# Weights and x of a hybrid decoder layer stored in HBM in the order in which SBUF holds them

## Chip, cores and metric

One core of one Trainium2 chip runs the kernel. The metric is the device time of one execution in microseconds (us). Three executions of the kernel before took 1139.64, 1139.92 and 1135.62 us, so the median is 1139.64 us. A fourth execution, the profiled one, took 1134.39 us; the trace is of that one, and its span from the first to the last instruction is 1132.3 us.

## What is computed

One decoder layer over 256 tokens of width 1024, in float32. A mixer with three groups of heads (gated linear attention, differential attention, retention) comes first, then a mixture of 32 experts of which each token takes four. Cut to what matters here:

```python
z = x @ w_in                                   # 1024 x 3344
a = concat(gla(z), diff_attention(z), retention(z)) @ w_out
x = layer_norm(alpha * x + a)
top_v, top_i = top_k(x @ w_router + b_router, 4)
for e in range(32):                            # for the tokens that chose e
    gu = x @ w_gate_up[e] + b_gate_up[e]       # 1024 x 2048
    g, u = min(gu[:, ::2], 7), clip(gu[:, 1::2], -7, 7)
    y += gate * (((u + 1) * g * sigmoid(1.702 * g)) @ w_down[e] + b_down[e])   # 1024 x 1024
ple = sigmoid(x @ w_ple_gate + b_ple_gate) * (p @ w_ple_proj)
out = layer_norm(alpha * x + y + ple)
```

`lay_out` rearranges inputs on the host, ahead of the launch; that is not in the measured time.

## The kernel before

**Units.** Every weight passes through a ring of 22 SBUF slots, each `[128, 2048]` float32, which is 1 MB: 8 KB in each of 128 partitions. A load of one slot is called a unit here. An expert has eight units of `w_gate_up`, `("gu", e, k)`, and four of `w_down`, `("dn", e, i)`. The mixer has 13 units of `w_in`, `("z", c)`, and four of `w_out`; `x` is one unit; the per-layer embedding (PLE) has four units of `w_ple_gate`, `("ple", i)`, and beside them four loads of 256 KB of `w_ple_proj`.

**Order.** `want` (L163) puts units into a list in the order in which they are to be loaded, `pump` (L170) gives the next of the list a slot whenever one is free, and `done` (L180) frees a slot after its last reader. All loads are issued by SyncE (SP) on one queue. The list is: `w_in` in the order of `zorder` (L262), `w_out`, `x`, then for expert after expert the eight units of `w_gate_up` of e and the four of `w_down` of e-1; with experts 9 to 12 the PLE units are mixed in. The transfers of one queue land in the order of their issue, some lines that the profile shows apart.

**Layout before.** `w_gate_up` is taken as it lies in HBM: row k*128+p of an expert has 2048 numbers, so partition p of a unit is one piece of 8 KB (`load_flat`, L243). The other weights have narrower rows, and a unit takes several rows for each partition:

- `load_rows2` (L221) for `w_down` and `w_out`: two pieces of 4 KB for each partition.
- `load_cols` (L211) for `w_in` and `load_colblock` (L228) for `w_ple_gate` and the first three units of the last expert's `w_down`: eight pieces of 1 KB.
- `load_cols` with `parts=2` for the second unit of `w_in` (`O_RG`), and `load_halves` (L235) for the last unit of the last `w_down`: halves of 512 KB in pieces of 512 bytes.
- `load_first_cols` (L269): the first unit of `w_in` (`O_GO`) and the transposed x (`xT`), in four quarters of 256 KB each, in turn, in pieces of 1 KB.

```python
            v = u.rearrange("p (k c) -> p k c", k=2)
            nc.sync.dma_start(v, src.rearrange("(k p) c -> p k c", p=P))
```

**Compute.** The mixer splits each `w_in` unit into two float32r parts (ACT, `split` L406; DVE, L407) and multiplies (L417, L418, L420, L432 to L435); its first unit goes unsplit (`z_unsplit`, L444). Nine matmuls on zeros run ahead of that (`keep_warm`, L381). Of the experts, `expert_up` (L1100) takes the eight `w_gate_up` units one after the other, eight matmul records for each, and frees each after its use; `expert_down` (L1127) does the same with the four units of `w_down`, eight records for each. The order in the loop is up(e), combining of a finished pair, down(e-1), activation of e. An expert with over 64 tokens takes an extra branch (`over_gather` L1143, `over_up` L1166). The last expert's `w_down` is taken by column blocks in `last_down` (L1406), each with its share of the final layer norm.

Of the kernel before, what the change touches and what calls it, by code (L numbers as in the profile page):

```python
# [69 lines left out]


def shape_constants():
    c = np.zeros((P, C_BIG), np.float32)
# [33 lines left out]
def lay_out(inp):  # L107
# [14 lines left out]
    for g in range(4):  # L122
# [4 lines left out]

    bgu = a["b_gate_up"][0].reshape(NE, 4, 2, P, 2).transpose(3, 4, 2, 1, 0)
    return {
        "x": a["x"], "xT": a["x"][0].T, "pT": a["p"][0, 0].T, "w_in": a["w_in"], "w_out": a["w_out"],  # L130
        "diff_lambda": a["diff_lambda"], "params": r, "bgu": bgu.reshape(P, 512),
        "w_gate_up": a["w_gate_up"], "w_down": a["w_down"], "b_down": a["b_down"],
        "w_ple_gate": a["w_ple_gate"], "w_ple_proj": a["w_ple_proj"],
        "ln2": np.concatenate([a["ln2_g"], a["ln2_b"]], axis=1), "big": big, "small": small, "lmask": lmask,
# [4 lines left out]
def kernel(ctx, tc, x, xT_in, pT_in, w_in, w_out, diff_lambda, params, bgu_in, w_gate_up,  # L139
                      w_down, b_down, w_ple_gate, w_ple_proj, ln2, big, small, lmask_in, out, debug=None):  # L140
    nc = tc.nc
# [65 lines left out]

    O_GQ, O_GV, O_GO, O_DQ, O_DK, O_DV = 0, 256, 528, 784, 1296, 1808
    O_RQ, O_RK, O_RV, O_RG = 2320, 2576, 2832, 3088
# [18 lines left out]
    def load_colblock(src):  # L228
        def fn(u):
            v = u.rearrange("p (k c) -> p k c", k=NK)  # L230
            nc.sync.dma_start(v, src.rearrange("(k p) c -> p k c", p=P))
            return v
        return fn

    def load_halves(src):  # L235
        def fn(u):
            v = u.rearrange("p (c w) -> p c w", c=8)
            for sl in (slice(0, 128), slice(128, 256)):
                nc.sync.dma_start(v[:, :, sl], src[:, sl].rearrange("(c p) w -> p c w", p=P))
            return v  # L240
        return fn
# [11 lines left out]
    def load_x(u):  # L253
        v = u.rearrange("p (t d) -> p t d", t=NT)
        nc.sync.dma_start(v, x[0].rearrange("(t p) d -> p t d", p=P))
        return v

    def load_ln2(u):
        nc.sync.dma_start(u[0:1, :], ln2)
        return u  # L260

    zorder = [O_GO, O_RG, O_GQ, O_RQ, O_RK, O_GV, O_RV, O_DQ, O_DK, O_DQ + 256, O_DK + 256, O_DV, O_DV + 256]  # L262

# [5 lines left out]
    def load_first_cols(u):  # L269

        v = u.rearrange("p (k c) -> p k c", k=NK)
        for q in range(4):
            sl, rows = slice(2 * q, 2 * q + 2), slice(256 * q, 256 * q + 256)
# [4 lines left out]
    for c in zorder:  # L278
        want(("z", c), load_first_cols if c == O_GO else load_cols(c, 2 if c == O_RG else 1))
        if c == O_RG:  # L280
            aside(lambda: load_first())
        if c == O_GQ:
            aside(lambda: load_second())
    for i in WORDER:
        want(("wo", i), load_rows2(w_out[0, i * 256:(i + 1) * 256, :]))
    want("xs", load_x)
# [4 lines left out]
    for e in range(NRUN + 1):  # L291
# [3 lines left out]
        if e >= 1:  # L295
            for i in range(4):
                sl = slice(i * 256, (i + 1) * 256)
                if e < NRUN:
                    fn = load_rows2(w_down[0, e - 1, sl, :])
                else:  # L300
                    fn = (load_halves if i == 3 else load_colblock)(w_down[0, e - 1, :, sl])
                units.append((("dn", e - 1, i), fn))
# [4 lines left out]
        if e in PLE_AT:  # L307
            i = PLE_AT.index(e)
            if i == 0:
                units += [("x1T", lambda u: u), ("plt", lambda u: load_pT(u))]  # L310
            units.append((("ple", i), load_colblock(w_ple_gate[0, :, i * 256:(i + 1) * 256])))
        for key, fn in units:
# [97 lines left out]
    def z_transposed(c):  # L410
        u = loaded["z", c].rearrange("p (k c) -> p k c", k=NK)
# [800 lines left out]
    def general():  # L1212

        n_max = load_count(cnt[0:1, NE:NE + 1])
        with tc.If(n_max > NSLOT + NOVER):
# [9 lines left out]
            with tc.For_i(0, NRUN, 1) as ie:  # L1225
# [3 lines left out]
                with tc.If(n > NSLOT + NOVER):  # L1229
                    with tc.For_i(0, (n - (NSLOT + 1)) // NOVER, 1):  # L1230
# [27 lines left out]
    def load_pT(u):  # L1258
        pT, w0, w1, sg = carve(u, (2, S), (2, 256), (2, 256), (2, S))
        nc.sync.dma_start(pT, pT_in.rearrange("(k p) t -> p k t", p=P))  # L1260
        return pT, (w0, w1), sg

    def load_proj(i):
        nc.sync.dma_start(loaded["plt"][1][i % 2],
                          w_ple_proj[0, :, i * 256:(i + 1) * 256].rearrange("(k p) c -> p k c", p=P))

# [133 lines left out]
    def last_down(c0, n):  # L1400
        w, o, h = loaded["dn", f, c0 // 256], c0 % 256, n // 2
        py = ps_z("pyl")
        for c in range(8):
            blk, j = c // 2, c % 2
            for hf in range(2):
                nc.tensor.matmul(py[hf * 64:(hf + 1) * 64, :h], act[:, j * 4 + blk, :],  # L1406
                                 w[:, c, o + hf * h:o + (hf + 1) * h], start=c == 0, stop=c == 7)
        nc.scalar.copy(y[64:128, c0:c0 + h], py[0:64, :h])
# [48 lines left out]
```

## Time and profile before

| what | value |
|---|---|
| median of three executions | 1139.64 us |
| profiled execution | 1134.39 us |
| its span | 1132.3 us |
| PE busy | 1038.6 us, 92% of the span |
| DVE, ACT busy | 396.5 us, 194.1 us |
| mean granted TensorE clock | 0.976 |
| moved by DMA | 433.61 MB, mean 383 GB/s |
| DMA packets | 100299: 33325 under 2 KB, 67409 under 8 KB |

PE is TensorE's matmul stream, and "idle before" in a row is the time in which the engine stood still ahead of it. The ends of matmuls are modelled: a group's last record is drawn some tenths of a microsecond past the point at which the next could start. DMA share is the mean busy share of the 16 DMA engines; it passes 1.00 where packets overlap. GB/s counts what they moved. A granted clock of 1.00 is 2.4 GHz, 0.50 is 1.2 GHz.

### The profile page before, as it was taken

To read this page: it belongs to the slowest core of one execution; us is meant where nothing else is said; L and a number is where in the kernel's file an instruction comes from. 1 tells how busy PE (TensorE), PEld (TensorE's weight loads), DVE (VectorE), ACT (ScalarE), POOL (GpSimd) and SP (SyncE) were. 2 spreads that over 40 slices of the span, in tenths; PEclk is the share of its full clock that TensorE was granted. 3 is DMA by queue.
4 is the path that set the end of the run, shared out by engine and by line. 5 is a ranking of instruction groups with operands and counts; after the bars stand their busy time and mean duration, and the time that the engine had idled before them with its cause. 6 is when DMAs were issued, how large, how long until landed. Compare 5 with 4: busy or idle time off the path is not lost. (4 is left out here: it accounts for less than half of the span.)

```text
span 1132.3 us, 13655 instructions
## 1 busy us (share of the span) xinstructions
PE 1038.6 (92%) x5358; PEld 515.0 (45%) x5358; DVE 396.5 (35%) x809; ACT 194.1 (17%) x377; POOL 7.5 (1%) x19
## 2 busy tenths in 40 slices
PE   9999989999999989999899999799988799999996
PEld 7988844433433354554433343234322343334344
DVE  4977642333333241232223233223232223232235
ACT  4457431101110120101101111001010110102011
POOL 1000000000000000000000000000000000000000
PEclk9999999999999999999999999899999799999998
DMA  9956877999999999999999999999999999999991
GB/s 316 359 235 258 319 312 278 415 416 414 417 416 417 416 404 406 407 411 411 417 416 417 415 417 415 415 416 416 415 416 417 415 417 401 386 416 416 415 373 58
DMA packets 100299, 433.61 MB, mean 383 GB/s; under 512 B 6957, under 2 KB 33325, under 8 KB 67409
## 3 DMA queue, kind: packets, MB, share of 16 engines
q1 hardware_dynamic: 100002, 431.36, 95.3%
q8 instruction: 88, 1.44, 0.5%
q0 software_dynamic: 176, 0.53, 0.1%
q14 instruction: 33, 0.27, 0.1%
HBM read 430.81 MB, written 1.06 MB: 381 GB/s over the span
## 5 line engine op out<-in xcount | busy, mean ns | idle before, releaser
L1100 PE MATMUL pgu<-u,xe 128*64 128x512 f32 x2048 | 475.5, 604 | 15.4 <-DMA u<-in_w_gate_up_dram 8.9
L1100 PEld LDWEIGHTS pgu<-u,xe 128*64 128x64 f32 x2048 | 161.1, 139 | 307.1 <-issue 271.4
L1127 PE MATMUL py<-u,u 128*64 128x512 f32 x992 | 234.9, 605 | 27.8 <-DVEq L1361 18.0
L1127 PEld LDWEIGHTS py<-u,u 128*64 128x64 f32 x992 | 79.6, 139 | 166.7 <-issue 125.0
L1109 DVE COPY u<-pgu 128x512 f32<-128x512 f32 x32 | 22.1, 692 | 332.1 <-PE pgu L1100 330.8
L1055 DVE TENSOR_TENSOR u<-ptg,bgu 128x512 f32<-128x512 f32 x32 | 22.1, 692 | 236.7 <-PE ptg L1115 236.7
L1108 ACT COPY u<-pgu 128x512 f32<-128x512 f32 x32 | 18.7, 585 | 449.1 <-PE pgu L1100 430.2
L1132 ACT COPY u<-py 64x512 f32<-64x512 f32 x31 | 17.9, 578 | 277.7 <-PE py L1127 277.7
L407 DVE TENSOR_TENSOR u<-u,u 128x1024 fp32r<-128x1024 f32 x32 | 39.0, 1222 | 17.5 <-ACT u L406 17.5
L1090 DVE TENSOR_TENSOR u<-u,pcb 128x512 f32<-128x512 f32 x60 | 37.7, 682 | 13.9 <-PE pcb L1089 13.8
L406 ACT CAST u<-u 128x1024 fp32r<-128x1024 f32 x32 | 33.5, 1048 | 29.6 <-PE pzt L418 9.7
L417 PE MATMUL pzt<-u,u 128*128 128x256 f32 x128 | 32.8, 291 | 0.3 <-ACT u L406 0.3
L1276 PE MATMUL pleg<-u,u 128*128 128x256 f32 x128 | 31.0, 397 | 2.1 <-ACT u L972 2.1
L418 PE MATMUL pzt<-u,u 128*128 128x256 f32 x128 | 32.3, 287 | 0.0
L1089 PE MATMUL pcb<-u,PT 128*128 128x512 f32 x120 | 32.0, 408 | 0.0
L1022 PE MATMUL pgx<-Pm,xnh 128*128 128x256 f32 (+1 forms) x128 | 30.9, 284 | 0.0
L1115 PEld LDWEIGHTS ptg<-ci,u 128*128 128x128 f32 x128 | 17.8, 207 | 27.7 <-issue 26.9
L1022 PE MATMUL pgx<-Pm,xnl 128*128 128x256 f32 (+1 forms) x128 | 30.0, 278 | 0.0
L1276 PEld LDWEIGHTS pleg<-u,u 128*128 128x128 f32 x128 | 24.9, 199 | 6.3 <-ACT u L972 2.2
L1057 ACT ACTIVATE u<-u 128x512 f32<-128x512 f32 x32 | 19.9, 623 | 44.1 <-DVE u L1056 44.1
L1022 PEld LDWEIGHTS pgx<-Pm,xnh 128*128 128x128 f32 x128 | 24.1, 188 | 6.5 <-issue 4.1
L1089 PEld LDWEIGHTS pcb<-u,PT 128*128 128x128 f32 x120 | 21.0, 188 | 11.7 <-ACT u L1108 4.9
(290 smaller groups left out, 954.9 us busy)
## 6 DMA issues: line engine op xcount, KB each, us to landing
u<-in_w_gate_up_dram SPq DMA_DIRECT2D x256, 1024.0 KB, 18.7
u<-in_w_down_dram SPq DMA_DIRECT2D x127, 1024.0 KB, 20.0
u<-in_w_in_dram SPq DMA_DIRECT2D x11, 1024.0 KB, 12.6
u<-in_w_out_dram SPq DMA_DIRECT2D x4, 1024.0 KB, 10.8
u<-in_w_ple_gate_dram SPq DMA_DIRECT2D x4, 1024.0 KB, 20.6
u<-in_xT_dram SPq DMA_DIRECT2D x4, 256.0 KB, 4.7
u<-in_w_in_dram SPq DMA_DIRECT2D x4, 256.0 KB, 4.7
u<-in_w_in_dram SPq DMA_DIRECT2D x2, 512.0 KB, 7.5
```

The costliest lines, as they stand in the source:

```text
L406: nc.scalar.copy(wh, half)
L407: nc.vector.tensor_tensor(wl, half, wh.bitcast(F32), op=ALU.subtract)
L417: nc.tensor.matmul(pz[:, j, :], wh[:, k, :], xh[:, k, :], start=k == 0, stop=False)
L418: nc.tensor.matmul(pz[:, j, :], wh[:, k, :], xl[:, k, :], start=False, stop=False)
L1022: nc.tensor.matmul(pg[:, j, :n], v[:, t, ch], hot, start=t + i == 0, stop=t + i == NT)
L1055: nc.vector.tensor_tensor(g, pg, bg, op=ALU.add)
L1089: nc.tensor.matmul(pcb, PT[:, t * P:(t + 1) * P], v[:, sl], start=i == 0, stop=i == 1)
L1090: nc.vector.tensor_tensor(yacc[:, t, sl], yacc[:, t, sl], pcb, op=ALU.add)
L1100: nc.tensor.matmul(pgu[b][hf * 64:(hf + 1) * 64, :], xe[:, k, c0:c0 + NSLOT], w[:, b * 1024 + hf * 512:b * 1024 + (hf + 1) * 512], start=k ...
L1109: nc.vector.tensor_copy(gs[:, 1, :], pgu[1])
L1127: nc.tensor.matmul(py[nb * 64:(nb + 1) * 64, :], act[:, j * 4 + blk, :], w[:, f % 2, nb * 512:(nb + 1) * 512], start=f == 0, stop=f == 7)
L1276: nc.tensor.matmul(pg[:, j, :], w[:, k, sl], x1T[:, k, :], start=k == 0, stop=k == NK - 1)
```

## The change

Every transfer of a weight or of x becomes one piece for each partition. `lay_out` stores each unit as a `[128, 2048]` block, partition after partition, so a unit is 1 MB in one run of HBM, 8 KB for each partition. The halves of the second `w_in` unit and of the last `w_down` unit become blocks of 4 KB for each partition, the quarters of `xT` and of the first `w_in` unit, and the loads of `pT` and `w_ple_proj`, 2 KB for each partition. The transposed `w_in` units are stored by column halves, so that `split` reads 1024 numbers in a row where it read eight runs of 128; what lies in the slots is otherwise the same. The last expert's `w_down` is stored a second time, by columns (`w_last`). `w_gate_up`, the constants and the small parameters stay as they are. The number of loads, their sizes and their order stay, too.

```diff
+    by_rows = lambda m, n: m.reshape(-1, n, P, m.shape[-1]).transpose(0, 2, 1, 3).reshape(-1, P, n * m.shape[-1])
+    cols = lambda m, c, n: by_rows(m[:, c:c + n], m.shape[0] // P)[0]
+    halves = lambda m, c: np.concatenate([cols(m, c, P), cols(m, c + P, P)], axis=1)
...
-        "w_gate_up": a["w_gate_up"], "w_down": a["w_down"], "b_down": a["b_down"],
-        "w_ple_gate": a["w_ple_gate"], "w_ple_proj": a["w_ple_proj"],
+        "w_gate_up": a["w_gate_up"], "w_down": np.stack([by_rows(w, 2) for w in a["w_down"][0]]),
+        "w_last": np.stack([cols(w_last, 256 * i, 256) for i in range(3)] + [halves(w_last, 768)]),
+        "b_down": a["b_down"],
+        "w_ple_gate": np.stack([cols(w_pg, 256 * i, 256) for i in range(4)]),
+        "w_ple_proj": np.stack([cols(w_pp, 256 * i, 256) for i in range(4)]),
...
-    def load_cols(c0, parts):
+    def load_cols(c, parts):
         def fn(u):
-            v = u.rearrange("p (k c) -> p k c", k=NK)
-            src = w_in[0, :, c0:c0 + 256].rearrange("(k p) c -> p k c", p=P)
-            n = 256 // parts
+            n, src = 2048 // parts, w_in[ZORDER.index(c)]
             for i in range(parts):
-                nc.sync.dma_start(v[:, :, i * n:(i + 1) * n], src[:, :, i * n:(i + 1) * n])
+                nc.sync.dma_start(u[:, i * n:(i + 1) * n], src[:, i * n:(i + 1) * n])
             return u
         return fn
...
-    def load_rows2(src):
+    def load_blocks(src, k):
         def fn(u):
-            v = u.rearrange("p (k c) -> p k c", k=2)
-            nc.sync.dma_start(v, src.rearrange("(k p) c -> p k c", p=P))
-            return v
-        return fn
...
+            nc.sync.dma_start(u, src)
+            return u.rearrange("p (k c) -> p k c", k=k)
...
-            nc.sync.dma_start(xT[:, sl, :], xT_in[rows].rearrange("(k p) t -> p k t", p=P))
-            nc.sync.dma_start(v[:, sl, :], w_in[0, rows, O_GO:O_GO + 256].rearrange("(k p) c -> p k c", p=P))
+            nc.sync.dma_start(xu[:, sl], xT_in[:, sl])
+            nc.sync.dma_start(u[:, sl], w_in[ZORDER.index(O_GO)][:, sl])
...
-                    fn = load_rows2(w_down[0, e - 1, sl, :])
+                    fn = load_blocks(w_down[e - 1, i], 2)
...
-        parts = [split(u[:, :, j * P:(j + 1) * P]) for j in range(2)]
+        parts = [split(u[:, j]) for j in range(2)]
```

The order of instructions is the same on every engine; only the shapes of SP's loads differ. SP's first loads before (`u_69` is `xT`, `u_95` the unit `O_GO`, `u_104` the unit `O_RG`):

```order
5 L274 DMA u_69<-in_xT_dram 128x2x256
6 L275 DMA u_95<-in_w_in_dram 128x2x256
7 L274 DMA u_69<-in_xT_dram 128x2x256
8 L275 DMA u_95<-in_w_in_dram 128x2x256
9 L217 DMA u_104<-in_w_in_dram 128x8x128 x2
```

and of the change:

```order
5 L277 DMA u_69<-in_xT_dram 128x512
6 L278 DMA u_95<-in_w_in_dram 128x512
7 L277 DMA u_69<-in_xT_dram 128x512
8 L278 DMA u_95<-in_w_in_dram 128x512
9 L231 DMA u_104<-in_w_in_dram 128x1024 x2
```

Each load keeps its place and its size, and its second dimension (the pieces of a partition) is gone. The same on SP where expert 9's `w_down` and the first PLE loads stand, before:

```order
163 L224 DMA u_4009<-in_w_down_dram 128x2x1024
164 L1338 UNCONDITIONAL_BRANCH
165 L224 DMA u_4015<-in_w_down_dram 128x2x1024
166 L224 DMA u_4021<-in_w_down_dram 128x2x1024
167 L224 DMA u_4027<-in_w_down_dram 128x2x1024
168 L1260 DMA u_4038<-in_pT_dram 128x2x256
169 L231 DMA u_4105<-in_w_ple_gate_dram 128x8x256
```

and of the change:

```order
163 L238 DMA u_4009<-in_w_down_dram 128x2048
164 L1339 UNCONDITIONAL_BRANCH
165 L238 DMA u_4015<-in_w_down_dram 128x2048
166 L238 DMA u_4021<-in_w_down_dram 128x2048
167 L238 DMA u_4027<-in_w_down_dram 128x2048
168 L1262 DMA u_4038<-in_pT_dram 128x512
169 L238 DMA u_4105<-in_w_ple_gate_dram 128x2048
```

Nothing moved; two pieces of 1024 numbers became one of 2048, and eight pieces of 256 one of 2048.

## Rows read from the trace of the kernel before

**Rows 1.** The page's 40 slices (28.3 us each): DMA share, GB/s

```profile
DMA  9956877999999999999999999999999999999991
GB/s 316 359 235 258 319 312 278 415 416 414 417 416 417 416 404 406 407 411 411 417 416 417 415 417 415 415 416 416 415 416 417 415 417 401 386 416 416 415 373 58
```

**Rows 2.** Stretches: us, busy of PE, PEld, DVE, ACT, POOL; PEclk, DMA share, GB/s

```profile
0.00:194.50 194.50, 185.24 (x1258) 142.43 (x1260) 116.92 (x289) 88.05 (x187) 7.48 (x19) 0.99 0.82 296
...
400.00:811.00 411.00, 376.99 (x1752) 175.45 (x1749) 119.88 (x219) 47.13 (x83) 0.00 (x0) 0.98 1.02 413
811.00:885.00 74.00, 61.87 (x268) 19.85 (x264) 15.62 (x28) 5.94 (x10) 0.00 (x0) 1.00 1.02 417
904.00:958.00 54.00, 49.63 (x306) 20.78 (x299) 16.48 (x37) 5.05 (x9) 0.00 (x0) 1.00 1.02 417
```

**Rows 3.** PE in order of time: start, us, what, count, [idle before <-releaser]

```profile
396.23 1.94 PE L1100 MATMUL pgu<-u,xe 128*64 128x512 f32 x8 [0.55 <-DMA u<-in_w_gate_up_dram]
...
717.38 1.94 PE L1100 MATMUL pgu<-u,xe 128*64 128x512 f32 x8 [0.56 <-DMA u<-in_w_gate_up_dram]
...
834.16 1.94 PE L1100 MATMUL pgu<-u,xe 128*64 128x512 f32 x8 [0.56 <-DMA u<-in_w_gate_up_dram]
836.64 1.94 PE L1100 MATMUL pgu<-u,xe 128*64 128x512 f32 x8 [0.54 <-DMA u<-in_w_gate_up_dram]
...
846.84 7.09 PE L1127 MATMUL py<-u,u 128*64 128x512 f32 x32 [1.23 <-DVEq L1361]
...
882.58 1.94 PE L1127 MATMUL py<-u,u 128*64 128x512 f32 x8 [0.61 <-DMA u<-in_w_down_dram]
```

**Rows 4.** PE's waits from 811 to 885 us: total us, times, longest

```profile
PE pgu L1100 <- DMA u<-in_w_gate_up_dram: 5.4, 9, 1.0
PE py L1127 <- DMA u<-in_w_down_dram: 4.2, 8, 0.6
```

**Rows 5.** PE's waits from 885 us to the end, the two largest

```profile
PE pox L1143 <- DVE Pr L965: 5.4, 1, 5.4
PE py L1127 <- DVEq L1361: 4.3, 3, 1.6
```

**Rows 6.** Stretches with pieces of 8, 4, 8, 4 and 1 KB alone

```profile
285.50:302.50 17.00, 15.43 (x86) 8.66 (x84) 5.42 (x10) 2.84 (x5) 0.00 (x0) 1.00 1.02 421
306.00:312.50 6.50, 5.47 (x32) 2.31 (x28) 3.07 (x6) 1.21 (x2) 0.00 (x0) 1.00 1.03 410
...
546.50:560.00 13.50, 11.76 (x54) 3.56 (x50) 0.00 (x0) 0.49 (x1) 0.00 (x0) 1.00 1.01 417
...
467.00:472.00 5.00, 3.04 (x16) 2.17 (x17) 1.98 (x3) 0.47 (x1) 0.00 (x0) 1.00 1.02 409
...
24.00:45.00 21.00, 21.00 (x173) 20.13 (x172) 18.69 (x48) 11.02 (x18) 2.34 (x2) 1.00 1.10 349
```

**Rows 7.** SP's loads: count, KB each, median us to landing

```profile
u<-in_w_gate_up_dram SPq DMA_DIRECT2D x256, 1024.0 KB, 18.7
```

**Rows 8.** PE, then ACT, in the first 16 us, in order of time

```profile
1.17 4.02 PE L381 MATMUL pwm<-u 128*128 128x512 bf16 x9 [1.17 <-DVE u L384]
4.98 7.67 PE L444 MATMUL pzu<-u,u 128*128 128x256 f32 x32
12.93 0.39 PE L417 MATMUL pzt<-u,u 128*128 128x256 f32 x1 [0.28 <-ACT u L406]
...
11.83 1.04 ACT L406 CAST u<-u 128x1024 fp32r<-128x1024 f32 x1 [1.96 <-DMA u<-in_w_in_dram]
```

**Rows 9.** Line 406: ns min/median/max, first and last start, form

```profile
L406 ACT CAST u<-u x32: 1033/1047/1075, 11.8 to 130.8; 128x1024 fp32r<-128x1024 f32 x32
```

**Rows 10.** SP in order of time, a PLE load pair

```profile
463.64 9.61 SPq L1264 DMA_DIRECT2D u<-in_w_ple_proj_dram  x1
```

**Rows 11.** The two stretches at the lower clock, as in rows 2

```profile
890.00:904.00 14.00, 12.43 (x60) 8.26 (x64) 1.08 (x4) 2.26 (x8) 0.00 (x0) 0.51 1.02 410
...
958.00:966.00 8.00, 8.00 (x19) 2.35 (x19) 2.20 (x5) 0.00 (x0) 0.00 (x0) 0.57 0.77 307
```

More of the change, by code (lines that the diff above doesn't have):

```diff
@@ L69 @@
 R_ALL = R_RBROW + 32
+O_GQ, O_GV, O_GO, O_DQ, O_DK, O_DV = 0, 256, 528, 784, 1296, 1808
+O_RQ, O_RK, O_RV, O_RG = 2320, 2576, 2832, 3088
+ZORDER = (O_GO, O_RG, O_GQ, O_RQ, O_RK, O_GV, O_RV, O_DQ, O_DK, O_DQ + 256, O_DK + 256, O_DV, O_DV + 256)
+NATURAL = (O_GV, O_RV, O_DV, O_DV + 256)
 def shape_constants():
@@ L128, in lay_out @@
     bgu = a["b_gate_up"][0].reshape(NE, 4, 2, P, 2).transpose(3, 4, 2, 1, 0)
+    by_rows = lambda m, n: m.reshape(-1, n, P, m.shape[-1]).transpose(0, 2, 1, 3).reshape(-1, P, n * m.shape[-1])
+    cols = lambda m, c, n: by_rows(m[:, c:c + n], m.shape[0] // P)[0]
+    halves = lambda m, c: np.concatenate([cols(m, c, P), cols(m, c + P, P)], axis=1)
+    w_in, w_last, w_pg, w_pp = a["w_in"][0], a["w_down"][0, NE - 1], a["w_ple_gate"][0], a["w_ple_proj"][0]
     return {
-        "x": a["x"], "xT": a["x"][0].T, "pT": a["p"][0, 0].T, "w_in": a["w_in"], "w_out": a["w_out"],
-        "diff_lambda": a["diff_lambda"], "params": r, "bgu": bgu.reshape(P, 512),
-        "w_gate_up": a["w_gate_up"], "w_down": a["w_down"], "b_down": a["b_down"],
-        "w_ple_gate": a["w_ple_gate"], "w_ple_proj": a["w_ple_proj"],
+        "x": by_rows(a["x"][0], NT)[0], "xT": by_rows(np.ascontiguousarray(a["x"][0].T), NK)[0],
+        "pT": by_rows(np.ascontiguousarray(a["p"][0, 0].T), 2)[0],
+        "w_in": np.stack([(cols if c in (O_GO, *NATURAL) else halves)(w_in, c, *([256] if c in (O_GO, *NATURAL) else []))
+                          for c in ZORDER]),
+        "w_out": by_rows(a["w_out"][0], 2),
+        "diff_lambda": a["diff_lambda"], "params": r, "bgu": bgu.reshape(P, 512),
+        "w_gate_up": a["w_gate_up"], "w_down": np.stack([by_rows(w, 2) for w in a["w_down"][0]]),
[3 more added lines that the diff above has]
+        "w_ple_proj": np.stack([cols(w_pp, 256 * i, 256) for i in range(4)]),
         "ln2": np.concatenate([a["ln2_g"], a["ln2_b"]], axis=1), "big": big, "small": small, "lmask": lmask,
@@ L139 @@
 def kernel(ctx, tc, x, xT_in, pT_in, w_in, w_out, diff_lambda, params, bgu_in, w_gate_up,
-                      w_down, b_down, w_ple_gate, w_ple_proj, ln2, big, small, lmask_in, out, debug=None):
+                      w_down, w_last, b_down, w_ple_gate, w_ple_proj, ln2, big, small, lmask_in, out, debug=None):
     nc = tc.nc
@@ L236, in fn @@
         def fn(u):
[L237 to L240, printed above, removed]
+            for sl in (slice(0, 1024), slice(1024, 2048)):
+                nc.sync.dma_start(u[:, sl], src[:, sl])
+            return u.rearrange("p (h c w) -> p c h w", h=2, c=8)
         return fn
@@ L253, in load_x @@
     def load_x(u):
-        v = u.rearrange("p (t d) -> p t d", t=NT)
-        nc.sync.dma_start(v, x[0].rearrange("(t p) d -> p t d", p=P))
-        return v
+        nc.sync.dma_start(u, x)
+        return u.rearrange("p (t d) -> p t d", t=NT)
     def load_ln2(u):
@@ L269, in load_first_cols @@
     def load_first_cols(u):
-        v = u.rearrange("p (k c) -> p k c", k=NK)
+        xu = xT.rearrange("p k t -> p (k t)")
         for q in range(4):
-            sl, rows = slice(2 * q, 2 * q + 2), slice(256 * q, 256 * q + 256)
-            nc.sync.dma_start(xT[:, sl, :], xT_in[rows].rearrange("(k p) t -> p k t", p=P))
-            nc.sync.dma_start(v[:, sl, :], w_in[0, rows, O_GO:O_GO + 256].rearrange("(k p) c -> p k c", p=P))
+            sl = slice(512 * q, 512 * q + 512)
+            nc.sync.dma_start(xu[:, sl], xT_in[:, sl])
+            nc.sync.dma_start(u[:, sl], w_in[ZORDER.index(O_GO)][:, sl])
         return u
-    for c in zorder:
+    for c in ZORDER:
         want(("z", c), load_first_cols if c == O_GO else load_cols(c, 2 if c == O_RG else 1))
@@ L284 @@
     for i in WORDER:
-        want(("wo", i), load_rows2(w_out[0, i * 256:(i + 1) * 256, :]))
+        want(("wo", i), load_blocks(w_out[i], 2))
     want("xs", load_x)
@@ L296 @@
             for i in range(4):
-                sl = slice(i * 256, (i + 1) * 256)
                 if e < NRUN:
-                    fn = load_rows2(w_down[0, e - 1, sl, :])
+                    fn = load_blocks(w_down[e - 1, i], 2)
                 else:
-                    fn = (load_halves if i == 3 else load_colblock)(w_down[0, e - 1, :, sl])
+                    fn = load_halves(w_last[i]) if i == 3 else load_blocks(w_last[i], NK)
                 units.append((("dn", e - 1, i), fn))
@@ L310 @@
                 units += [("x1T", lambda u: u), ("plt", lambda u: load_pT(u))]
-            units.append((("ple", i), load_colblock(w_ple_gate[0, :, i * 256:(i + 1) * 256])))
+            units.append((("ple", i), load_blocks(w_ple_gate[i], NK)))
         for key, fn in units:
@@ L1400, in last_down @@
     def last_down(c0, n):
-        w, o, h = loaded["dn", f, c0 // 256], c0 % 256, n // 2
+        w, h = loaded["dn", f, c0 // 256], n // 2
+        w = w[:, :, c0 % 256 // P] if n == P else w
         py = ps_z("pyl")
@@ L1406, in last_down @@
                 nc.tensor.matmul(py[hf * 64:(hf + 1) * 64, :h], act[:, j * 4 + blk, :],
-                                 w[:, c, o + hf * h:o + (hf + 1) * h], start=c == 0, stop=c == 7)
+                                 w[:, c, hf * h:(hf + 1) * h], start=c == 0, stop=c == 7)
         nc.scalar.copy(y[64:128, c0:c0 + h], py[0:64, :h])
```

19 lines of the change are left out of this document (5 added, 14 removed).

## The prediction, made blind

> **What bounds the kernel now.** I read the slices first: the rate of the transfers is uneven for seven slices, 235 to 359 GB/s, and from the eighth on (198 us) almost flat at 404 to 417 GB/s until the end, with the share of the 16 DMA engines at its top [rows 1]. The stretches say the same: up to 194.5 us the DMA engines are busy 0.82 of the time, from 400 us on 1.02 [rows 2]. So the queue is starved of free slots in the mixer and the first experts, where TensorE sets the pace (185 of 194.5 us busy), and from 194.5 us to the last load it never runs dry.
>
> A queue that is never dry need not bound anything, since the ring can hold units that TensorE does not want yet. So the next view is PE in order of time, and PE's waits. Where TensorE is ahead, its eight records of a unit start 2.48 us after the last eight (834.16 to 836.64 us), each time released by the landing; where it is not, it needs (7.09 - 1.94) / 3 = 1.72 us for a unit, from the four units in the row at 846.84 us [rows 3]. The reader should see two things. First, TensorE catches up with the transfers in three places: three waits around 396 us, four around 717 us, and seventeen between 811 and 885 us [rows 3, 4]. Secondly, the last such wait ends at 882.58 us [rows 3]; of the nine kinds of wait that PE has after 885 us none is for a DMA; the two largest are for DVE's index work ahead of an overflowing expert and at a branch [rows 5].
>
> Thus the run has three parts: to 194.5 us TensorE's pace; to 882.6 us the transfers' pace, since whatever TensorE did in between, it stood waiting for a landing at 882.6; and then some 250 us at TensorE's pace again. **What a faster transfer gives is counted from 194.5 to 882.6 us and nowhere else.**
>
> **The change, part by part.** The sum is made against the profiled execution's 1134.39 us.
>
> *`w_down`, two pieces of 4 KB to one of 8 KB.* The trace has both sizes in one queue. Stretches with 8 KB pieces alone ran at 421 and 417 GB/s, weighted 419.2; those with 4 KB alone at 410 and 409, weighted 409.6 [rows 6]. A unit of 1.0486 MB takes 2.501 us at the one and 2.560 us at the other: 0.059 us saved. The loads from `dn` 2 to `dn` 23 lie between the two marks, 22 x 4 = 88 units: 88 x 0.059 = 5.2 us. Ends: 417 against 410 gives 0.043 us and 3.8 us; 421 against 409 gives 0.073 us and 6.4 us. The new block is read just as a `w_gate_up` unit is, 8 KB for each partition in one run of 1 MB, so I take the 8 KB rate as it stands.
>
> *PLE.* Four units and five loads of 256 KB go from 1 KB to 8 KB and 2 KB. Their stretches are mixed with others, so the price of 1 KB is taken from the `w_in` loads, 349 GB/s or 3.00 us a unit [rows 6]: 4 x (3.00 - 2.50) = 2.0 us. For the 1.25 MB in small loads, between 0 (2 KB no better than 1 KB) and 0.6 us (as good as 8 KB); I take the middle, 0.3 us. The slices give a second price: the five with PLE run at 404, 406, 407, 411 and 411 GB/s where their neighbours run at 417 [rows 1], short by 46 x 28.3 / 417 = 3.1 us in all. Together 2.3 us, ends 2.0 and 3.1.
>
> *The first microseconds.* TensorE spends 1.17 to 5 us on matmuls on zeros, then 7.67 us on 16 unsplit products in 32 records, stands 0.28 us, and starts the second unit at 12.93 us, when ACT has split what landed at 11.8 us [rows 8]. The eight quarters and the first 512 KB half land sooner with larger pieces, but TensorE can't start before its zeros are done, and the 32 records need most of those 7.67 us for themselves. Bounds: 0, and 1.0 us (the 0.28 us and the little by which the records are spread). I take 0.6 us, nearer to the visible wait and some of the spread. It shifts the whole first part, so it adds to the rest.
>
> *What costs nothing.* The rest of `w_in`, `w_out` and `x`, 16 units, lands faster and lies in the first part, under TensorE's pace; if that cover were gone (TensorE faster there), some 0.5 us for each `w_in` unit would be gained, so it is no loss in any case. `w_last` lies behind 885 us, where PE waits for no DMA [rows 5]; it can only land sooner. SP's own instructions get cheaper, as a PLE load of 256 KB held SP for 9.61 us [rows 10], and still the queue didn't run dry, because a unit lands 18.7 us after its issue [rows 7] at 2.5 us for each, some seven in flight. ACT's split takes 1033 to 1075 ns over 32 instructions, strided and contiguous halves alike [rows 9], so the new storage order of the halves gives nothing. No instruction is added or moved, so no wait is new.
>
> *Sum.* 5.2 + 2.3 = 7.5 us to 882.6 us, plus 0.6: 8.1 us, ends 5.8 and 10.5. TensorE must be able to follow. It had 3 + 4 + 17 = 24 waits of about 2.48 - 1.72 = 0.76 us, some 18 us, and the transfers give back 7.5; it will still stand waiting near 882.6, with fewer waits, and what is late next there is still `w_down` and `w_gate_up`. So 1134.39 - 8.1 = 1126.3 us for an execution like the profiled one. That one was 5.25 us under the median of 1139.64; at the median, **1131.5 us**.
>
> The Trainium skill speaks against this sum: its page "DMA: Bandwidth & Descriptors", section "Rules for kernel authors", wants 128 partitions and at least 1 MiB for each DMA, and nothing more, for most of the bandwidth. All the units had that before, so by the rule the change would bring next to nothing (rival 1, its second case); the trace disagrees, since units of one size differ by 2% with the piece [rows 6].
>
> **The rivals.** A difference of 0.5% (5.7 us) is about what a measurement can tell from no change.
>
> *1. Only part of `w_down`'s lower rate belongs to the piece.* A 4 KB stretch always follows a switch from one tensor to another, which stays. If half of the 2% stays, `w_down` gives 2.6 us, and with half of PLE and the same start 2.6 + 1.2 + 0.6 = 4.4 us: 1135.2 us, no change that can be told. If all of it stays, in PLE too, 0.6 us is left: 1139.0 us, which is the case of the rule above. Against both: both rates hold flat over stretches of 5 to 17 us, and the 1 KB stretch lies in line (349) [rows 6]. The Trainium skill, "DMA: Bandwidth & Descriptors", section "Why small descriptors are slow (HBM only)", names a fixed overhead of about three bus cycles a descriptor at 32 bytes a cycle; worked out from that, as an estimate, two pieces of 4 KB cost 262 cycles against 259, 1.2%, and 88 units would give 2.6 us. By the rows the price is twice that.
>
> *2. TensorE becomes the bound before 882.6 us.* It has some 10 us in hand (18 against 7.5). Spells at the lower clock could use that up; 20 us more at 1.2 GHz would, and each 2 us beyond take 1 us of the gain. For it: 0.98 mean clock from 400 to 811 us [rows 2]. A case in its middle keeps half, 4 us: 1135.6 us.
>
> *3. Slower: the clock.* After 885 us the run goes at TensorE's pace, and there two stretches, 14.0 us at 0.51 and 8.0 us at 0.57 [rows 11], lie around the overflowing expert, where TensorE had stood for 5.4 us waiting for DVE [rows 5]. Together they cost 14.0 x 0.49 + 8.0 x 0.43 = 10.3 us. If the shifted arrivals leave other gaps there and the clock comes back later, every us more at 1.2 GHz costs half a us: 16 us more eat the gain, 28 us more make the kernel slower by 0.5%, 1145 us with 28. Against it: the work from 885 us on is the same, and from 904 to 958 us it ran at 1.00 [rows 2].
>
> *4. More.* If TensorE has less to wait for, it may also lose fewer spells, and 8 KB at 421 GB/s without the switch would make it 10 to 12 us: 1128.5 us.
>
> That the pieces don't become larger is excluded by the shapes of SP's loads.
>
> **How the numbers follow.** The forecast 0.72, rival 1 0.11 (0.02 of it for nothing at all), rival 2 0.05, rival 3 0.04, rival 4 0.08. The forecast's own range is its ends, 1139.64 - 10.5 = 1129.1 to 1139.64 - 5.8 = 1133.8 us; its lower end moves to 1124.5 us if executions come out as the profiled one did (1126.3, and a little below), its upper to 1136 us with rivals 1 and 2. So 1124.5 to 1136 us. Faster by over 0.5% (under 1133.9 us): most of the forecast (0.68), rival 4 and a little of rivals 1 and 2, 0.77; within 0.5% 0.19; slower 0.04, rival 3.
>
> **What would show it.** In the profile after: packets under 8 KB fall from 67409 to under 14000; the GB/s digits are flat near 419 from the eighth slice on, without the dip at PLE; waits of PE for DMA remain between 800 and 885 us, fewer than seventeen, the last ending near 874 us; the stretch from there to the end is as long as before, some 250 us. I am wrong if the flat rate stays at 410 in `w_down`'s stretches (rival 1), if PE has no DMA wait after 700 us (rival 2), or if the stretch behind the last wait grew (rival 3).

## The result and the profile after

| | before | change |
|---|---|---|
| median of seven executions each, side by side | 1139.63 us | 1129.34 us |
| lowest and highest | 1133.74, 1139.92 us | 1128.16, 1130.85 us |
| profiled execution, its span | 1134.39, 1132.3 us | 1130.51, 1128.5 us |

The ratio, taken over the executions side by side, is 0.9924, with a 95% interval of 0.9905 to 0.9943: about 8.7 us (6.5 to 10.8), where 8.1 us were forecast. The two medians lie 10.3 us apart; that of the kernel before stands near the top of its seven executions here, and in the later series it is 1136.0 to 1138.2 us. The change's median lies 2.2 us under the 1131.5 us forecast, well inside the range. The two traced executions differ by 3.9 us only: that of before was near the low end of its kernel's scatter, that of the change in the upper half of its own. So what follows compares stretches of traces, and times only as ratios.

The page of the change, its slices and its packets, to be read against [rows 1]:

```profile
GB/s 350 365 199 226 314 304 282 404 420 420 420 419 420 419 419 419 419 420 403 420 407 421 419 420 420 418 419 420 419 420 420 420 421 408 403 419 421 420 351 38
DMA packets 62411, 433.61 MB, mean 384 GB/s; under 512 B 6957, under 2 KB 7469, under 8 KB 10705
```

Packets under 8 KB fell from 67409 to 10705. From the ninth slice on the rate stands at 418 to 421 GB/s, but for the slices from 930 us on that were low before, too, and two lone slices, 403 and 407, which are new and are taken up further down. The dip of the five PLE slices, 404 to 411, is gone.

The stretches of [rows 2], and then two short ones with `w_gate_up` alone and `w_down` alone, as in [rows 6]; columns as there:

```profile
0.00:194.50 194.50, 184.84 (x1244) 142.89 (x1244) 117.61 (x288) 88.02 (x187) 7.41 (x19) 0.98 0.77 294
400.00:811.00 411.00, 378.90 (x1770) 177.96 (x1768) 119.89 (x219) 47.26 (x83) 0.00 (x0) 0.98 1.01 418
811.00:885.00 74.00, 61.24 (x272) 21.74 (x268) 20.15 (x36) 8.05 (x13) 0.00 (x0) 0.99 1.01 420
...
605.20:621.30 16.10, 15.70 (x72) 6.61 (x68) 7.00 (x12) 1.83 (x3) 0.00 (x0) 1.00 1.01 419
624.30:631.70 7.40, 6.37 (x34) 2.67 (x30) 1.72 (x3) 0.58 (x1) 0.00 (x0) 1.00 1.02 418
```

From 400 to 811 us the DMA share is about what it was, 1.01 against 1.02; it now carries 418 GB/s instead of 413, and `w_down` runs as `w_gate_up` does. In landings: the median spacing of a `w_down` unit was 2.548 us and is 2.487 us, that of a `w_gate_up` unit stays at 2.49 us.

PE's waits from 811 to 885 us, then from 885 us to the end, as [rows 4] and [rows 5]:

```profile
PE pgu L1102 <- DMA u<-in_w_gate_up_dram: 3.8, 6, 1.1
PE py L1129 <- DMA u<-in_w_down_dram: 2.2, 4, 0.6
...
PE pox L1145 <- DVE Pr L967: 5.4, 1, 5.4
PE py L1129 <- DVEq L1362: 4.3, 3, 1.6
```

Ten waits for transfers are left of seventeen (thirteen in a second trace of the change), and those around 396 and 717 us [rows 3] are gone. Behind 885 us the same two waits lead, to the tenth. PE in order of time, the end of the stretch that the transfers bound, as [rows 3]:

```profile
834.17 1.94 PE L1102 MATMUL pgu<-u,xe 128*64 128x512 f32 x8 [0.54 <-DMA u<-in_w_gate_up_dram]
836.65 1.94 PE L1102 MATMUL pgu<-u,xe 128*64 128x512 f32 x8 [0.55 <-DMA u<-in_w_gate_up_dram]
...
841.87 7.09 PE L1129 MATMUL py<-u,u 128*64 128x512 f32 x32 [1.23 <-DVEq L1362]
...
877.73 1.94 PE L1129 MATMUL py<-u,u 128*64 128x512 f32 x8 [0.53 <-DMA u<-in_w_down_dram]
```

The last wait for a landing ends at 877.73 us, where it ended at 882.58. TensorE still stands waiting for `w_down` there, so the transfers still bound the run up to that point.

Where did it come from? I measure from the landing of the second `w_gate_up` unit of expert 3, behind which at least two loads are always under way, to the landing of the last `w_down` unit of expert 23, the one that this last wait waits for: 684.25 us before, 675.87 us after. That is 8.4 us gained between 200 and 880 us. The span shrank by less, because 3.5 us were lost ahead of that stretch and 1.0 us behind it (882.58 to 1132.3 is 249.7 us, 877.73 to 1128.5 is 250.8). These two losses are those of this pair of traces: in a second pair, further down, that first landing is only 0.8 us later. Of the 3.5 us, 0.8 us show in the first microseconds and some 1.7 us, half of 3.4, are a spell at 1.2 GHz in the mixer, shown in the last section; the rest is open. The first microseconds, PE and then ACT, as [rows 8]:

```profile
4.98 2.75 PE L446 MATMUL pzu<-u,u 128*128 128x256 f32 x8
8.15 5.42 PE L446 MATMUL pzu<-u,u 128*128 128x256 f32 x24 [0.42 <-DMA u<-in_w_in_dram]
13.72 0.39 PE L419 MATMUL pzt<-u,u 128*128 128x256 f32 x1
...
10.44 0.62 ACT L391 CAST u<-u 128x512 fp32r<-128x512 f32 x1 [1.13 <-DMA u<-in_xT_dram]
12.62 1.05 ACT L408 CAST u<-u 128x1024 fp32r<-128x1024 f32 x1 [1.57 <-DMA u<-in_w_in_dram]
```

TensorE starts the second `w_in` unit at 13.72 us, not at 12.93, and ACT's first split, 11.83 us before, starts at 12.62 us: what the eight quarters bring lands later, with pieces twice as large. Behind the last wait, too, there is a spell at 1.2 GHz that the trace of the kernel before does not have, 3.4 us long and so worth some 1.7 us (columns as in [rows 2]):

```profile
1016.50:1021.00 4.50, 4.50 (x16) 1.29 (x14) 0.00 (x0) 0.09 (x1) 0.00 (x0) 0.62 1.01 421
```

### The profile page after: what moved, and what is told of

It reads as the page before. It is cut to its first block, busy times and chain, and to the rows that moved or that the text cites. A ratio compares the mean times of both kernels' runs of the same rounds, so it can differ in the third digit from the quotient of the medians.

```text
span 1128.5 us, 13655 instructions
## 1 busy us (share of the span) xinstructions
PE 1041.2 (92%) x5358; PEld 520.7 (46%) x5358; DVE 397.3 (35%) x809; ACT 194.1 (17%) x377; POOL 7.4 (1%) x19
## 5 line engine op out<-in xcount | busy, mean ns | idle before, releaser
L1102 PE MATMUL pgu<-u,xe 128*64 128x512 f32 x2048 | 473.3, 603 | 10.6 <-DMA u<-in_w_gate_up_dram 4.1
L1129 PE MATMUL py<-u,u 128*64 128x512 f32 x992 | 236.5, 608 | 25.8 <-DVEq L1362 16.7
L419 PE MATMUL pzt<-u,u 128*128 128x256 f32 x128 | 34.0, 299 | 0.1
L420 PE MATMUL pzt<-u,u 128*128 128x256 f32 x128 | 33.6, 296 | 0.0
## 6 DMA issues: line engine op xcount, KB each, us to landing
u<-in_w_gate_up_dram SPq DMA_DIRECT2D x256, 1024.0 KB, 16.7
u<-in_w_last_dram SPq DMA_DIRECT2D x3, 1024.0 KB, 20.5
```

The source lines that it names most:

```text
L1102: nc.tensor.matmul(pgu[b][hf * 64:(hf + 1) * 64, :], xe[:, k, c0:c0 + NSLOT], w[:, b * 1024 + hf * 512:b * 1024 + (hf + 1) * 512], start=k ...
L1129: nc.tensor.matmul(py[nb * 64:(nb + 1) * 64, :], act[:, j * 4 + blk, :], w[:, f % 2, nb * 512:(nb + 1) * 512], start=f == 0, stop=f == 7)
```

## The experiments

Two theories stood against each other. **Mine:** a unit's time depends on the size of its pieces, wherever it stands in the queue, and what is saved from 200 to 880 us is the gain. **The rival:** a `w_down` stretch is slower because the queue switches tensors there, or because of which tensor it is. The late start was a third question. The experiments came in three groups, each with its own executions of the kernel before beside it.

**`w_down` alone**, on the kernel before:

```diff
+        "w_down": np.stack([by_rows(w, 2) for w in a["w_down"][0]]), "w_last": a["w_down"][0, NE - 1],
...
-                    fn = load_rows2(w_down[0, e - 1, sl, :])
+                    fn = load_blocks(w_down[e - 1, i], 2)
```

> Only w_down of experts 0 to 30 is stored in blocks of 8 KB for each partition; all else as before. Theory (the piece sets the rate, and only loads between 194.5 and 882.6 us count): 88 units x 0.059 us = 5.2 us less than before, and w_down's stretches run at the rate of w_gate_up's, 417 to 421 GB/s. Rival (part of w_down's lower rate comes from the switch between tensors): at most half, 2.6 us, with w_down's stretches below 415 GB/s. Both: the dip of the rate at PLE stays, and the first landings are those of before.

Measured: median 1130.1 us of seven, ratio 0.9932 (0.9908 to 0.9956). DMA packets fall by 15872, which is 128 for each of the 124 units: one packet for each piece. The landings from expert 3 to expert 23 span 679.62 us, 4.6 us less than before. Two stretches, `w_gate_up` and then `w_down`:

```profile
607.10:623.10 16.00, 14.78 (x68) 5.91 (x66) 3.31 (x6) 0.59 (x1) 0.00 (x0) 1.00 1.02 421
626.10:633.60 7.50, 7.14 (x34) 2.54 (x36) 4.40 (x10) 0.63 (x1) 0.00 (x0) 1.00 1.03 423
```

and its slices:

```profile
GB/s 316 359 239 254 322 308 255 407 421 420 419 420 420 418 409 411 411 418 406 420 420 421 418 421 418 420 420 420 419 421 421 421 420 396 389 419 421 420 367 40
```

With 8 KB pieces `w_down` runs at `w_gate_up`'s rate although the switch between the tensors is still there. The PLE dip (409, 411, 411) stays, as it should.

**PLE alone**, on the kernel before:

```diff
+        "w_ple_gate": np.stack([cols(a["w_ple_gate"][0], 256 * i, 256) for i in range(4)]),
+        "w_ple_proj": np.stack([cols(a["w_ple_proj"][0], 256 * i, 256) for i in range(4)]),
...
-            units.append((("ple", i), load_colblock(w_ple_gate[0, :, i * 256:(i + 1) * 256])))
+            units.append((("ple", i), load_blocks(w_ple_gate[i], NK)))
```

> Only w_ple_gate, w_ple_proj and the transposed p are stored in blocks; all else as before. Theory: 2.3 us less than before (2.0 to 3.1), w_down's stretches stay at 410 GB/s, a PLE unit lands some 0.4 to 0.5 us sooner behind the last. Rival: half of that, 1.2 us. Either is within what a measurement can tell from no change; the stretch from the first landing after the queue was last dry to the last wait of PE for a landing should be shorter by the same 2.3 us.

Measured: median 1134.08 us of twelve, ratio 0.9971 (0.9953 to 0.9988); the landings span 681.72 us, 2.5 us less than before. The slices lose the dip, and stay below 419 elsewhere:

```profile
GB/s 312 358 241 239 316 309 278 417 415 416 416 417 417 416 416 415 415 415 417 416 411 417 416 417 415 414 415 417 415 416 417 418 416 401 389 416 417 415 372 59
```

**The front alone**: the change with `w_down`, PLE, `pT` and the last expert's loads as before.

```diff
-                    fn = load_blocks(w_down[e - 1, i], 2)
+                    fn = load_rows2(w_down[0, e - 1, i * 256:(i + 1) * 256, :])
```

> Only w_in, w_out, x and the transposed x are stored in blocks; all else as before. Theory of the prediction: 0.6 us less than before. Rival, from the profile after (second quarter of x landed at 7.3 us where it was 6.3, and TensorE reached its second w_in unit 0.8 us later): the quarters of 2 KB pieces land later, so the kernel is 0.8 to 1.1 us longer than before. Both: between the first landing after the queue was last dry and the last wait of PE for a landing the same time as before, 684 us.

Measured: median 1138.48 us of twelve, ratio 1.0019 (1.0001 to 1.0037). The landings from expert 3 on span 684.31 us, as before. So the layout of `w_in`, `w_out`, `x` and `xT`, as the change has it, brings nothing and costs a little, some 2 us with an interval from 0.1 to 4.2. PE and ACT in its first microseconds:

```profile
4.98 6.54 PE L460 MATMUL pzu<-u,u 128*128 128x256 f32 x24
12.08 1.97 PE L460 MATMUL pzu<-u,u 128*128 128x256 f32 x8 [0.55 <-DMA u<-in_w_in_dram]
14.32 0.39 PE L433 MATMUL pzt<-u,u 128*128 128x256 f32 x1 [0.28 <-ACT u L422]
...
11.30 0.62 ACT L405 CAST u<-u 128x512 fp32r<-128x512 f32 x1 [2.33 <-DMA u<-in_xT_dram]
```

The last quarter landed so late that TensorE waited for it inside the first unit. The ratios add up: 0.68% of 1138.22 us is 7.7 us gained with `w_down`, 0.29% is 3.3 us with PLE, 0.19% is 2.2 us lost at the front, together 8.9 us; the change has 8.7 us.

**The change with the old quarters**: the eight first loads as before, from `xT` and `w_in` rows, in pieces of 1 KB.

```diff
-            nc.sync.dma_start(xu[:, sl], xT_in[:, sl])
-            nc.sync.dma_start(u[:, sl], w_in[ZORDER.index(O_GO)][:, sl])
+            nc.sync.dma_start(xT[:, sl, :], xT_in[rows].rearrange("(k p) t -> p k t", p=P))
+            nc.sync.dma_start(v[:, sl, :], w_raw[0, rows, O_GO:O_GO + 256].rearrange("(k p) c -> p k c", p=P))
```

> The change with the first eight loads alone (the quarters of the transposed x and of the first w_in unit) as before, in pieces of 1 KB. If the larger pieces are what made the quarters land later, the second quarter of x lands at 6.3 us as before, TensorE starts its second w_in unit at 12.9 us or earlier, and the kernel takes 0.8 us less than the change. If the later landing was chance, the landings scatter here too and the time is that of the change.

Measured: median 1128.42 us of six, ratio 0.9924 (0.9898 to 0.9951), which is the change's own ratio: in the time this is inconclusive. The trace does tell: the second unit starts at 12.76 us.

```profile
7.54 5.42 PE L446 MATMUL pzu<-u,u 128*128 128x256 f32 x24 [0.86 <-DMA u<-in_w_raw_dram]
12.76 0.38 PE L419 MATMUL pzt<-u,u 128*128 128x256 f32 x1
```

**`w_gate_up` in two pieces of 4 KB**, on the change. It gives the other tensor the small pieces, and doubles the count of such units.

```diff
-            units += [(("gu", e, k), load_flat(w_gate_up[0, e, k * P:(k + 1) * P, :])) for k in range(NK)]
+            units += [(("gu", e, k), load_two(w_gate_up[e, k])) for k in range(NK)]
...
+            nc.sync.dma_start(u.rearrange("p (h c) -> p h c", h=2), src.rearrange("h p c -> p h c"))
```

> The change with w_gate_up stored so that each unit has two pieces of 4 KB for each partition, 512 KB apart, as w_down had before. Theory (each further piece of a partition costs a unit some 0.06 us, whatever the tensor): 22 experts x 8 units x 0.06 = 10.6 us longer than the change, so about as long as before; w_gate_up's stretches fall from 419 to 410 GB/s and w_down's stay at 419. Rival (the lower rate comes from the switch to w_down, not from the piece): w_gate_up's stretches stay at 417 to 421 GB/s and the time stays within 3 us of the change.

Measured: median 1142.45 us of ten, ratio 1.0051 (1.0025 to 1.0076). The landings span 687.78 us, 11.9 us more than the change (10.6 were expected); a `w_gate_up` unit takes 2.561 us. `w_gate_up`, then `w_down`:

```profile
641.70:658.30 16.60, 16.45 (x78) 6.88 (x76) 6.14 (x10) 3.13 (x5) 0.00 (x0) 1.00 1.03 411
661.30:668.80 7.50, 7.50 (x46) 4.32 (x43) 1.24 (x2) 1.62 (x3) 0.00 (x0) 1.00 1.01 416
```

The lower rate went over to `w_gate_up` together with the pieces. With that the rival falls: neither the switch nor the tensor makes the rate.

**`w_down` in four pieces of 2 KB**, on the change:

```diff
-                    fn = load_blocks(w_down[e - 1, i], 2)
+                    fn = load_pieces(w_down[e - 1, i])
...
+            nc.sync.dma_start(u.rearrange("p (h c) -> p h c", h=4), src.rearrange("h p c -> p h c"))
```

> The change with w_down in four pieces of 2 KB for each partition. Theory: three further pieces at 0.06 us each make a unit 0.18 us longer, 2.67 us or 392 GB/s; 88 units x 0.18 = 16 us longer than the change, some 6 us longer than before. Rival: the price of a piece is not the same for each, and a unit of 2 KB pieces lies anywhere between that of 4 KB (2.55 us) and of 1 KB (2.9 us): 5 to 35 us longer than the change.

Measured: median 1148.22 us of four, ratio 1.011 (1.0073 to 1.0147). The landings span 693.9 us, 18.0 us more than the change (16 were expected); a `w_down` unit takes 2.694 us. `w_gate_up`, then `w_down`:

```profile
645.70:661.90 16.20, 16.05 (x78) 6.75 (x76) 6.15 (x10) 3.13 (x5) 0.00 (x0) 1.00 1.02 419
664.90:673.60 8.70, 8.70 (x55) 5.97 (x52) 2.74 (x5) 2.85 (x5) 0.00 (x0) 1.00 1.05 396
```

PE's waits from 811 to 900 us:

```profile
PE py L1135 <- DMA u<-in_w_down_dram: 6.6, 9, 1.2
PE pgu L1108 <- DMA u<-in_w_gate_up_dram: 4.7, 9, 0.6
```

The price per unit goes with the count of pieces: one 2.487 us, two 2.548, four 2.694; 0.061 us for the second piece and 0.073 us for each of the next two. In these runs each further piece of a partition also lies elsewhere in HBM, 512 or 256 KB from the last; a price of the piece and one of that jump were not told apart. TensorE waits the longer for just that tensor, and the time follows.

**The late loads alone**: on the kernel before, only the `w_down` of experts 24 to 30, whose use lies behind the last wait for a transfer.

```diff
-                    fn = load_rows2(w_down[0, e - 1, sl, :])
+                    fn = load_blocks(w_late[e - 25, i], 2) if e > 24 else load_rows2(w_down[0, e - 1, sl, :])
```

> The kernel before with w_down of experts 24 to 30 alone in blocks of 8 KB. Theory (behind the last wait of PE for a landing, at 882.6 us, TensorE sets the pace): 0 us, though 28 units land 0.06 us sooner each; PE's last wait for a landing stays at dn 23. Rival (transfers set the pace to the end): 28 x 0.06 = 1.7 us less than before.

Measured: median 1137.56 us of twelve, ratio 1.0003 (0.9978 to 1.0027). In the time this is inconclusive: the interval reaches from 2.5 us of gain to 3.1 us of loss and so holds the rival's 1.7 us, too. The trace does tell. PE's last wait for a landing stays at the last unit of `dn` 23, at 883.24 us, and from 885 us on PE has no wait for a transfer, so there the edit that is worth 0.061 us a unit ahead of 880 us has no wait to shorten. That last wait for a landing, and the two largest waits behind 885 us:

```profile
883.24 1.94 PE L1136 MATMUL py<-u,u 128*64 128x512 f32 x8 [0.62 <-DMA u<-in_w_down_dram]
...
PE pox L1152 <- DVE Pr L974: 5.4, 1, 5.4
PE py L1136 <- DVEq L1370: 4.3, 3, 1.6
```

**The quarters as runs**, on the change: pieces of 2 KB for each partition as in the change, but each quarter of 256 KB is one run of HBM. In the change a quarter takes 2 KB out of every 8 KB of its block.

```diff
+    quarters = lambda m: m.reshape(P, 4, 512).transpose(1, 0, 2)
...
-            nc.sync.dma_start(xu[:, sl], xT_in[:, sl])
-            nc.sync.dma_start(u[:, sl], w_in[ZORDER.index(O_GO)][:, sl])
+            nc.sync.dma_start(xu[:, sl], xT_in[q])
+            nc.sync.dma_start(u[:, sl], w_first[q])
```

> The change with each quarter of the transposed x and of the first w_in unit stored as one run of 256 KB (2 KB for each partition, one after the other) in place of 2 KB out of every 8 KB. If the gaps between the pieces made the quarters land late, they land as before or sooner (second quarter of x by 6.3 us, TensorE's second w_in unit by 12.9 us) and the kernel takes 0.8 to 1.1 us less than the change. If it was the size of the pieces, or chance, TensorE starts that unit at 13.7 us or later.

Measured: median 1127.29 us of six, ratio 0.9911 (0.9884 to 0.9938). PE:

```profile
4.98 8.01 PE L447 MATMUL pzu<-u,u 128*128 128x256 f32 x32
12.64 0.47 PE L420 MATMUL pzt<-u,u 128*128 128x256 f32 x1
```

The second unit starts at 12.64 us instead of 13.72, with the same pieces in the same number: it was the gaps between them. In the time it can't be told from the change, 0.9911 against 0.9924. ACT's wait for the last quarter of `xT` ends at 9.05 us, where the change had 10.44.

**Every load a run**: the same for the halves of the second `w_in` unit and of the last `w_down` unit.

```diff
+    runs = lambda m: m.reshape(P, 2, 1024).transpose(1, 0, 2)
...
+        "w_rg": runs(halves(w_in, O_RG)), "w_end": runs(halves(w_last, 768)),
...
-                nc.sync.dma_start(u[:, sl], src[:, sl])
+                nc.sync.dma_start(u[:, sl], src[i])
```

> The run of quarters stored as runs of 256 KB, and the halves of the second w_in unit and of the last w_down unit stored as runs of 512 KB too, so that every load reads one run of HBM. Theory (gaps between the pieces delay the first loads): TensorE reaches its second w_in unit at 12.6 us as with the quarters alone or up to 0.3 us sooner, and the kernel takes 1 to 2 us less than the change. Rival (the quarters' gain was chance): the time of the change.

Measured: median 1125.77 us of six, ratio 0.9902 (0.9875 to 0.9928), the fastest median of all, though not told apart in the time from the quarters alone (0.9911). Its executions lie between 1123.91 and 1127.86 us; those of the change beside it, which follow, begin at 1128.23 us. The landings from expert 3 on span 675.54 us, as in the change (675.87), and the first expert's matmuls start at 150.31 us, where the change has 153.16: most of what it has over the change in the traces is won at the front. Some 1.7 us of that is the change's spell at 1.2 GHz near 82 us, which this trace doesn't have; the gaps alone show as 12.29 instead of 13.72 us.

```profile
7.22 5.42 PE L449 MATMUL pzu<-u,u 128*128 128x256 f32 x24 [0.40 <-DMA u<-in_w_first_dram]
12.29 0.47 PE L422 MATMUL pzt<-u,u 128*128 128x256 f32 x1
```

**The change and the kernel before once more**, unaltered, to have a second trace of each.

> The change itself again, for another trace of it and for a comparison on the chip on which the run with all loads in one run of HBM is timed. The second w_in unit starts at 13.7 us or later again if the gaps between 2 KB pieces delay it; the stretch from the first landing after the queue was last dry to PE's last wait for a landing takes 676 us again; 7 to 9 us less than before.

> The kernel before again, unchanged: how far two series of one kernel differ, and a second trace of it. The ratio should be within 0.25% of 1; the second w_in unit starts at 12.9 us, TensorE's first expert matmul between 150.3 and 152.3 us, and the stretch of transfers takes 684 us.

Measured: the change 1129.43 us of eleven, ratio 0.9945 (0.9924 to 0.9966), 6.3 us, which is less than the 7 to 9 us expected, though the interval (3.9 to 8.6) reaches into them; the kernel before 1137.77 us of twelve, ratio 1.0002 (0.9983 to 1.0021). The last waits for a transfer, and the start of the second `w_in` unit, first of the change, then of the kernel before:

```profile
13.95 0.39 PE L419 MATMUL pzt<-u,u 128*128 128x256 f32 x1 [0.28 <-ACT u L408]
...
877.06 1.94 PE L1129 MATMUL py<-u,u 128*64 128x512 f32 x8 [0.56 <-DMA u<-in_w_down_dram]
```

```profile
12.53 0.38 PE L417 MATMUL pzt<-u,u 128*128 128x256 f32 x1
...
885.30 1.94 PE L1127 MATMUL py<-u,u 128*64 128x512 f32 x8 [0.62 <-DMA u<-in_w_down_dram]
```

The stretch from expert 3 to 23 comes out again, at 675.41 and 684.43 us, so 9.0 us. The late start comes out again, too. The part behind the last wait does not: it took 246.8 us in this trace of the kernel before (885.30 to 1132.1), 249.5 us in this one of the change, with the same work in it. Spells at 1.2 GHz make part of that: from 883 to 1026 us this trace of the kernel before has two of them, 17.1 us together, and the other three traces have 20.5 us (the first of the kernel before), 20.5 (this one of the change) and 23.9. Each microsecond of them costs half a microsecond, so they account for 1.7 of the 2.7 us here.

## Why the prediction was right, and where not

**What bounds the run: right.** The transfers bound it from 200 to 880 us, and besides only in the first microseconds, as taken up below. What was made faster between 200 and 880 us counted; behind it PE waits for no transfer, and the same edit there gave a ratio of 1.0003, too coarse to show 1.7 us by itself. The layout of the front gave no gain.

**`w_down`, 5.2 us: right in kind.** The price of a unit, taken from four short stretches as 0.059 us, is 0.061 us by the landings, and 88 units are 5.4 us. Whether a piece or its jump in HBM costs that is not told apart. Alone it gave 4.6 us in the trace and 7.7 us (5.0 to 10.5) in the time. Rival 1, that part of the rate belongs to the switch or the tensor, is refuted from both sides: `w_down` with large pieces rises to 423 GB/s, `w_gate_up` with small ones falls to 411.

The Trainium skill's page "DMA: Bandwidth & Descriptors" has two places on this. By its section "Rules for kernel authors", which asks for 128 partitions and at least 1 MiB for each DMA, units of 1 MiB had nothing more to gain; the unit that went from 2.548 to 2.487 us says otherwise. By its section "Why small descriptors are slow (HBM only)", with some three bus cycles for each packet, an estimate for four pieces against one is 268 to 259 cycles, 3.5%; measured are 2.694 to 2.487 us, 8.3%. The direction agrees, the price per piece is over twice the page's.

**PLE, 2.3 us: right.** 2.5 us in the trace, 3.3 us (1.4 to 5.3) in the time, and the dip went.

**The first microseconds, 0.6 us of gain: wrong, and in sign.** The step that failed is "the eight quarters and the first 512 KB half land sooner with larger pieces", and with it the lower bound of 0. The quarters land later. Over all traces the second unit starts at 13.7 to 14.3 us with quarters that take 2 KB out of every 8 KB (five traces, mean 14.0), at 12.5 to 13.3 us with the old ones (six traces, mean 12.8), at 12.64 and 12.29 us as runs. So the term is a loss of 1.2 us in place of a gain of 0.6. No row of the kernel before had a load of that shape, and I excluded a loss with no reason but the size of the pieces. The whole front cost 2.2 us (0.1 to 4.2) in the time.

**The sum, 8.1 us against 8.7: partly two errors that cancel.** By the ratios `w_down` and PLE gave 11.0 us where 7.5 were forecast, and the front lost 2.2 where 0.6 were to be gained. By the traces the stretch gained 8.4 to 9.0 us, and `w_down` and PLE alone 4.6 + 2.5 = 7.1 us; 1.3 to 1.9 us lie between. The landings show where. By the median spacings the units give 5.4 us for `w_down` and 2.1 us for PLE; the rest is delays that every trace has in this stretch, eight groups of up to some 2 us (the first, at 200 to 205 us, once 2.7), 80 to 110 us apart, each of one or a few landings that come late with at least two loads under way. Together they are 11.9 us before, 12.7 with `w_down` alone, 11.5 with PLE alone and 11.0 in the change. So `w_down` alone lost 0.8 us to them and the change won 0.9 us, and no further price of a piece is missing. What makes the delays is open.

**TensorE could follow: right, but nearer than I had it.** I counted 24 waits and 18 us in hand. Ten waits were left, thirteen in the second trace, and in two slices of the first the transfers no longer ran at the full rate: 403 and 407 GB/s, 28.2 x (17 + 13) / 420 = 2.0 us short. SP waits up to 9.1 us for a slot there, and three `w_gate_up` units issued there land 7.3 to 8.4 us later, where the median is 16.7, so the ring was full and the queue short. That is rival 2 in small, but TensorE lost little by it: the units behind the first dip land 2.5 us apart as elsewhere, and one behind the second comes 0.4 us late. No experiment was made on it.

**What would show it.** Packets under 14000: 10705. Flat near 419 without the dip: yes, but for the two lone slices. The last wait near 874 us: 877.7 and 877.1, since the front came late. Fewer than seventeen waits: ten and thirteen. The stretch behind: 250.8 and 249.5 us, where the kernel before has 249.7 and 246.8. By the sign that I gave, rival 3 may have come in small: by pairs of traces from 0.2 us less to 4.0 us more, of which spells at 1.2 GHz explain 0 to 3.4 us. That the change brings them is not shown: its second trace has as much of them as the first of the kernel before.

## What to carry to other kernels

Where a queue of transfers is never dry and its consumer waits for it, multiply the time per piece, read from the trace, by the pieces that lie in that stretch alone: here 0.06 to 0.07 us for every further piece per partition of a 1 MB unit. In such a stretch, storing a unit partition after partition is worth it even where the load is large already; but a load that takes only part of such a block should get a block of its own, in one run. A part of the sum for which the trace has no load of the new shape needs a bound on the side of a loss, too.

## What was not expected of the hardware

- **Gaps cost more than the size of the pieces.** The eight quarters, 2 MB in all, with 2 KB pieces: 13.7 to 14.3 us to the second unit when 6 KB are skipped behind each piece, 12.64 us when none is. Even 1 KB pieces were sooner, at 12.76 us (12.5 to 13.3 over six traces). What in the memory makes it so is open.
- **Most kernels with small pieces scatter more.** Twelve executions of the kernel before, in one group, lie between 1132.69 and 1140.17 us, ten with `w_gate_up` in 4 KB pieces between 1138.36 and 1147.28, twelve with the front alone between 1134.45 and 1142.33; six with every load a run within 4 us, 1123.91 to 1127.86, though two of eleven of the change stood at 1135.5 beside 1128 to 1130 otherwise, and twelve with PLE alone, whose `w_down` has pieces of 4 KB, lie within 5.5 us, 1131.68 to 1137.17. So that the pieces make the scatter is not shown. The traced executions of most kernels with small pieces were near their low ends, and no long one was traced, so where the additional microseconds lie is not known. That of `w_down` alone, 1131.24 us, was near the high end of its seven (1125.79 to 1131.9), which may be why it gained 7.7 us in the time and 4.6 us in the traces.
- **A spell at 1.2 GHz in the mixer.** Both traces of the change have one of some 3.4 us near 82 us, which those of the kernel before and of the last two variants don't have; PLE alone and the change with the old quarters have one of the same length near 52 us. Here the granted clock of the whole window is 0.57:

```profile
81.50:85.50 4.00, 4.00 (x22) 3.88 (x21) 2.69 (x16) 2.31 (x11) 0.00 (x0) 0.57 0.02 6
```

  TensorE was busy all through, and had stood for 0.74 us shortly before, up to 79.23 us. At half the clock 3.4 us cost some 1.7 us. A late start alone doesn't bring it: the front alone started latest of all, at 14.32 us, and stood at 1.00 from 80 to 110 us. What does is open.
